# The second table's last four tiles multiplied feature by feature, and another pace for the gathered rows' steps

## The chip, the cores and the metric

The kernel runs on one core of one Trainium2 chip. The metric is the device time of one execution in microseconds (us). Three runs of the kernel before gave 2100.40, 2096.53 and 2106.97 us; their median is 2100.4 us.

## The reference, cut to what matters

The program is two stacks one behind the other: two mixer layers, then two layers that each hold a mixer (HGRN2 in the first, RG-LRU in the second) and a PEER feed-forward part. The change touches the PEER part alone, which is computed twice, once per layer:

```
q = (h @ w_q) -> 8 heads, two halves each; scores against 128 sub-keys; top 16 of each half,
top 16 of their 256 sums: ids (16384 experts), gate = softmax(top_s)
u = u_tab[ids]; act = gelu(sum_d u * h)
out = sum over heads and the 16 picks of (gate * act) * v_tab[ids]
x = x + g2 * out
```

There are 256 tokens, 1024 features and two tables of 16384 x 1024 numbers (64 MB each) per layer. All data are float32.

## The kernel before, in words

Two ways of computing the PEER part stand side by side. For 160 of the 256 tokens (`TD`) it is dense: every tile of the tables is multiplied with all 160 tokens. For the other 96 (`TS`) only the picked rows are fetched, by indirect DMAs on GpSimd's queue, and VectorE multiplies and sums them.

**The second table's dense part** (line 1452). The table v is cut into 128 tiles of 128 experts. For tile j the kernel runs eight matmuls, one for each block c of 128 output features; each adds into a PSUM region of its own (`acc[c // 2][:, c % 2]`), its right operand is the 160 tokens' weights `W(j)`. In the trace one such float32 matmul shows as two records. Two tiles come in one load of 1 MB, called a pair here, on SyncE's queue into one of four buffers `w`; the load of a pair can be issued when the matmuls of the pair four before it are done.

**The gathered rows** (lines 1302 to 1332, `fetch` and `own`). Steps k = 0 to 95 gather rows of the first table, steps 96 to 191 rows of the second. One `fetch(k)` brings 128 rows (512 KB) into one of twelve buffers `r`; one `own(k)` on VectorE multiplies them with their weights and adds them to a sum `hl` of 128 x 1024. Each 32 steps fill one sum, so there are three in the second table: steps 96 to 127, 128 to 159 and 160 to 191. The first step of a sum is a plain product (line 1330), the other 31 are line 1332.

**The joins** (line 1446). When a sum is full, eight matmuls per join (16 records) add it, folded from slots to tokens, into the other 96 columns of the same PSUM regions. A join stands in TensorE's queue at a fixed place: `folds[j + 5]`, five tiles behind the tile at which its last step was written down. TensorE works in order, so a join that waits holds up every matmul behind it.

**The order.** The whole stage stands in `manual_schedule()`: instructions go out as written. The condition in line 1455, with the factor 122, says behind which tile j the next step k is written; and `fetch(k + 6, ends[j - 1])` lets the fetch start only when tile j - 1 is multiplied. With 122 the 96 steps go from tile 2 to tile 123, about one per 1.27 tiles, and the joins stand behind tiles 47 and 88 and behind the last tile.

**The end of the stage.** Behind the last join eight evictions (VectorE and ScalarE in turn, lines 1471 and 1473) take the PSUM regions to `hT` and scale them; sixteen transposes (line 1478) turn them back, four to a PSUM tile; four sums (line 363) add them to x. Then the next stage begins: the RG-LRU mixer behind the first PEER part, the final norm behind the second. The mixer's weight loads (`lruin`, `lruax`, line 243, into buffers `r`; `ada`, line 222, into buffers `w`) are issued on SyncE's queue as buffers come free.

Of the kernel before, what the change touches and what calls it, by code (L numbers as in the profile page):

```python
# [15 lines left out]
AF = mybir.ActivationFunctionType  # L16
ALU = mybir.AluOpType
AX = mybir.AxisListType

P = 128  # L20
# [7 lines left out]
TS = 96  # L28
# [109 lines left out]
class Kernel:  # L138
# [1053 lines left out]
    def peer(self, l):  # L1192
        from contextlib import ExitStack
        nc, tc, A = self.nc, self.tc, self.A
        pairs = {}

        def load(name, j):
            if j % 2 == 0:
                pairs[name] = self.slot(A[f"{name}{l}"][:, j * D:(j + 2) * D])
            return pairs[name][:, j % 2 * D:(j % 2 + 1) * D]  # L1200

        with ExitStack() as ctx:
            pool = lambda name, bufs=1, c=ctx: c.enter_context(tc.tile_pool(name=f"{name}{l}", bufs=bufs))
            pl = pool("pe")
            hT = self.t(pl, (P, 8, S), "hT")
# [100 lines left out]
            def fetch(k, behind=None):  # L1306

                if k < 2 * TS:
                    x = self.rp.tile([P, D], F32, name="r")
                    at = bass.IndirectOffsetOnAxis(ap=ids[:, k % TS:k % TS + 1], axis=0)  # L1310
                    g = nc.gpsimd.indirect_dma_start(out=x, out_offset=None, in_=A[f"urow{l}"] if k < TS else vrow,  # L1311
                                                     in_offset=at)
                    if behind is not None:
                        tc.add_manual_dep(g.ins, behind.name, mybir.DependencyInfo(
                            mybir.DependencyClass.Sync, mybir.DependencyReason.ANTI), reason="pace")
                    rows[k] = x

            def own(k):

                g, r = k % TS, k % TS // 32  # L1320
                x = rows.pop(k)
                if k < TS:
                    nc.vector.scalar_tensor_tensor(x, x, 1.0, hrep[r % 2], op0=ALU.mult, op1=ALU.mult,  # L1323
                                                   accum_out=asl[:, g:g + 1])
                    if k % 32 == 31:
                        gr = slice(32 * r, 32 * r + 32)
                        nc.scalar.activation(asl[:, gr], asl[:, gr], AF.Gelu_apprx_tanh)
                        nc.vector.tensor_tensor(asl[:, gr], asl[:, gr], gs[:, gr], op=ALU.mult)
                elif g % 32 == 0:
                    nc.vector.tensor_scalar(accs[r % 2], x, asl[:, g:g + 1], None, op0=ALU.mult)  # L1330
                else:
                    nc.vector.scalar_tensor_tensor(accs[r % 2], x, asl[:, g:g + 1], accs[r % 2], op0=ALU.mult,  # L1332
                                                   op1=ALU.add)

            with tc.manual_schedule():
                wts = {}

                def W(j):
                    return Wa[:, j] if j < JW else wts["b"][:, j - JW]
# [56 lines left out]
                k = 0  # L1396
                for j in range(P):
                    u_mm(j)
                    if j in (2, 29):
                        b = j // 29  # L1400
# [28 lines left out]
                    if j >= G0:  # L1429
                        n = j - G0  # L1430
# [10 lines left out]
                acc = [self.t(self.acc, (P, 2, S), "acc") for _ in range(4)]  # L1441
                ends, folds = [], {}

                def join(r):
                    for c in range(8):
                        nc.tensor.matmul(acc[c // 2][:, c % 2, :TS], accs[r % 2][:, c * P:(c + 1) * P], fold[:, r],  # L1446
                                         start=False, stop=r == NR - 1, skip_group_check=True)

                for j in range(P):
                    v = load("v", j)  # L1450
                    for c in range(8):
                        mm = nc.tensor.matmul(acc[c // 2][:, c % 2, TS:], v[:, c * P:(c + 1) * P], W(j),  # L1452
                                              start=j == 0 and c % 2 == 0, stop=False, skip_group_check=True)
                    ends.append(mm.ins)
                    if k < 2 * TS and (j - 2) * TS >= (k - TS) * 122:
                        own(k)
                        fetch(k + AHEAD, ends[j - 1])
                        k += 1
                        if k % 32 == 0:
                            folds[j + 5] = (k - TS) // 32 - 1  # L1460
                    if j in folds:
                        join(folds.pop(j))
                assert k == 2 * TS
                for r in folds.values():
                    join(r)

            g0 = 24 + 16
            for c in range(8):
                gate = self.mod[l][:, g0 + c:g0 + c + 1]
                if c % 2:  # L1470
                    nc.scalar.activation(hT[:, c], acc[c // 2][:, c % 2], AF.Copy, scale=gate)  # L1471
                else:
                    nc.vector.tensor_scalar(hT[:, c], acc[c // 2][:, c % 2], gate, None, op0=ALU.mult)  # L1473
            for b in range(2):
                for n in range(2):
                    ps = self.psum((P, 4, P))
                    for j in range(4):
                        nc.tensor.transpose(ps[:, j], hT[:, 4 * n + j, b * P:(b + 1) * P], self.ident)
                    self.add_x(b, n, ps.rearrange("p a b -> p (a b)"), None)

    def final(self, out):
        nc = self.nc
        rows = self.wp.tile([P, SLOT], F32, name="w")[:, :D]
        r = self.A["rows"]
        nc.scalar.dma_start(rows, bass.AP(tensor=r.tensor, offset=r.offset + R_FINAL, ap=[[0, P], [1, D]]))
        for b in range(2):
            o = self.rp.tile([P, D], F32, name="r")
            rs = self.rms_x(b)
            nc.vector.tensor_scalar(rs, rs, float(D) ** 0.5, None, op0=ALU.mult)
            nc.vector.scalar_tensor_tensor(o, self.x[:, b], rs, rows, op0=ALU.mult, op1=ALU.mult)  # L1490
            nc.sync.dma_start(out[b * P:(b + 1) * P], o)
# [38 lines left out]
```

## Time and profile before

| what | value |
|---|---|
| median of three runs | 2100.4 us |
| profiled execution, its own time | 2102.61 us |
| its span from first to last instruction | 2100.9 us |
| TensorE busy | 1998.1 us, 95% of the span |
| VectorE / ScalarE / GpSimd busy | 67% / 29% / 30% |
| granted TensorE clock, mean | 0.979 of full speed |
| line 1452 (second table, dense), both layers | 4096 records, 558.0 us |
| DMA | 630 MB, mean 300 GB/s |

How to read it: a group's row gives the time its records are on the engine, the mean duration of one, and behind the bar how long the engine stood idle just before them and what ended that. Matmul records overlap, so what one costs in a row of them is read from the chain of waits (time over count), not from its duration. The DMA share is the mean busy share of the 16 DMA engines.

### The profile page before, as it was taken

What the parts mean: (1) busy time and instruction counts of PE and PEld (TensorE: products, weight loads), DVE (VectorE), ACT (ScalarE), POOL (GpSimd) and SP (SyncE); (2) the same over time, 40 slices, a digit from 0 to 9 for tenths busy, and PEclk for the clock granted to TensorE, in tenths of its full rate; (3) what the DMA queues carried; (4) which work ended last, traced back from release to release, by engine and by line L of the source; (5) the groups of instructions that cost most, each with busy time, mean ns of one, the idle gap of its engine ahead of it and who ended that gap; (6) DMA issues with size and microseconds to landing.
All of it is one profiled execution on the core that took longest, in us unless ns stands there. A gap on an engine that the chain in (4) does not pass through costs nothing. (4 is left out here: it accounts for less than half of the span.)

```text
span 2100.9 us, 35398 instructions
## 1 busy us (share of the span) xinstructions
PE 1998.1 (95%) x13860; PEld 1871.6 (89%) x13860; DVE 1403.3 (67%) x3068; ACT 617.7 (29%) x1684; POOL 626.3 (30%) x683
## 2 busy tenths in 40 slices
PE   6997998999999989999999998999989999999997
PEld 6683795888769989999999998969989999999997
DVE  7698588577657777788444446976796788544344
ACT  4452472455433134433000002743224433000000
POOL 0201111011001564443343440001374444243442
PEclk9998999999999999999999998999999999999999
DMA  9647738442414999999999998643799999999996
GB/s 343 233 160 265 262 111 310 149 123 71 161 61 157 356 405 364 358 365 363 381 415 416 415 415 338 243 180 120 294 404 377 353 366 372 356 416 416 415 415 270
DMA packets 123719, 630.01 MB, mean 300 GB/s; under 512 B 13728, under 2 KB 14368, under 8 KB 79264
## 3 DMA queue, kind: packets, MB, share of 16 engines
q1 hardware_dynamic: 66960, 422.87, 52.5%
q0 software_dynamic: 55296, 201.35, 24.6%
q10 hardware_dynamic: 1296, 3.53, 0.5%
q8 instruction: 109, 1.79, 0.3%
q14 instruction: 58, 0.48, 0.1%
HBM read 626.65 MB, written 1.05 MB: 299 GB/s over the span
## 5 line engine op out<-in xcount | busy, mean ns | idle before, releaser
L1353 PE MATMUL ps<-hT,w 128*128 128x160 f32 x4096 | 574.8, 300 | 0.0
L1353 PEld LDWEIGHTS ps<-hT,w 128*128 128x128 f32 x4096 | 562.4, 191 | 0.0
L1332 DVE SCALAR_TENSOR_TENSOR hl<-r,asl,hl 128x1024 f32<-128x1024 f32 x186 | 239.0, 1285 | 314.8 <-DMA r<-v,ids 314.2
L1452 PE MATMUL acc<-Wa,w 128*128 128x160 f32 x2560 | 348.4, 299 | 0.0
L1452 PEld LDWEIGHTS acc<-Wa,w 128*128 128x128 f32 x2560 | 347.9, 190 | 0.0
L1311 POOL DMA_INDIRECT r<-v,ids x192 | 232.0, 1208 | 346.4 <-PE acc L1452 255.1
L1311 POOL DMA_INDIRECT r<-urow,ids x192 | 252.7, 1316 | 243.3 <-DVE r L1323 133.6
L1323 DVE SCALAR_TENSOR_TENSOR r<-r,hh 128x1024 f32<-128x1024 f32 x192 | 231.9, 1218 | 2.2 <-DMA r<-urow,ids 1.9
L1452 PE MATMUL acc<-Wb,w 128*128 128x160 f32 x1536 | 209.6, 299 | 0.2 <-DMA w<-v 0.2
L1452 PEld LDWEIGHTS acc<-Wb,w 128*128 128x128 f32 x1536 | 208.8, 190 | 0.5 <-DMA w<-v 0.5
L1471 ACT ACTIVATE hT<-acc,mod 128x256 f32<-128x256 f32 x8 | 3.7, 475 | 569.6 <-DVE hT L1473 569.6
L1373 ACT ACTIVATE r<-r,hl 128x128 f32<-128x128 f32 x320 | 102.3, 391 | 233.7 <-DVE r L1370 233.7
L257 PE MATMUL ps<-hh,r 128*128 128x256 f32 (+1 forms) x464 | 135.9, 293 | 4.6 <-ACT r L229 2.9
L259 PE MATMUL ps<-hh,r 128*128 128x256 f32 (+1 forms) x464 | 133.6, 288 | 6.6 <-DVE r L230 6.6
L258 PE MATMUL ps<-hl,r 128*128 128x256 f32 (+1 forms) x464 | 133.7, 288 | 1.0 <-DVE hl L381 1.0
L270 DVE SCALAR_TENSOR_TENSOR w<-w,crow 128x1024 f32<-128x1024 f32 x96 | 113.6, 1216 | 3.2 <-ACT crow L835 3.2
L230 DVE TENSOR_TENSOR r<-w,r 128x1024 fp32r<-128x1024 f32 (+1 forms) x82 | 97.5, 1199 | 27.2 <-ACT r L229 26.2
L229 ACT ACTIVATE r<-w 128x1024 fp32r<-128x1024 f32 (+1 forms) x82 | 84.3, 1039 | 77.8 <-PE ps L258 34.3
L1370 DVE TENSOR_TENSOR r<-cst,hl 128x1024 f32<-128x1024 f32 x80 | 97.4, 1218 | 0.0
L259 PEld LDWEIGHTS ps<-hh,r 128*128 128x128 f32 (+1 forms) x464 | 89.0, 192 | 7.9 <-DVE r L230 7.6
L257 PEld LDWEIGHTS ps<-hh,r 128*128 128x128 f32 (+1 forms) x464 | 89.5, 193 | 6.2 <-ACT r L229 3.8
L258 PEld LDWEIGHTS ps<-hl,r 128*128 128x128 f32 (+1 forms) x464 | 89.3, 193 | 2.1 <-DVE hl L381 1.6
(382 smaller groups left out, 2910.0 us busy)
## 6 DMA issues: line engine op xcount, KB each, us to landing
w<-u SPq DMA_DIRECT2D x128, 1024.0 KB, 8.0
w<-v SPq DMA_DIRECT2D x128, 1024.0 KB, 8.3
w<-ada SPq DMA_DIRECT2D x48, 1024.0 KB, 4.9
w<-win SPq DMA_DIRECT2D x24, 1024.0 KB, 5.0
r<-hgin SPq DMA_DIRECT2D x40, 512.0 KB, 4.4
w<-wq SPq DMA_DIRECT2D x12, 1024.0 KB, 5.0
r<-wout SPq DMA_DIRECT2D x16, 512.0 KB, 8.6
r<-wmid SPq DMA_DIRECT2D x12, 384.0 KB, 7.6
```

Source lines behind the costliest of these rows:

```text
L230: self.nc.vector.tensor_tensor(lo, x, hi.bitcast(F32), op=ALU.subtract)
L257: mm(ps, a[0], b[0], start=start, stop=False)
L258: mm(ps, a[0], b[1], start=False, stop=False)
L259: mm(ps, a[1], b[0], start=False, stop=stop)
L270: nc.vector.scalar_tensor_tensor(x, x, 1.0, self.cond, op0=ALU.mult, op1=ALU.mult, accum_out=m[:, j + i:j + i + 1])
L1311: g = nc.gpsimd.indirect_dma_start(out=x, out_offset=None, in_=A[f"urow{l}"] if k < TS else vrow, in_offset=at)
L1323: nc.vector.scalar_tensor_tensor(x, x, 1.0, hrep[r % 2], op0=ALU.mult, op1=ALU.mult, accum_out=asl[:, g:g + 1])
L1332: nc.vector.scalar_tensor_tensor(accs[r % 2], x, asl[:, g:g + 1], accs[r % 2], op0=ALU.mult, op1=ALU.add)
L1353: nc.tensor.matmul(ps, u[:, c], hT[:, c, TS:], start=c == 0, stop=c == 7)
L1370: nc.vector.tensor_tensor(o, self.iota[:, None, None].to_broadcast([P, 2, 4, P]), slots[:, 1:3, k:k + 4, None].to_broadcast([P, 2, 4, P]), ...
L1373: nc.scalar.activation(o[:, 1, t], o[:, 1, t], AF.Copy, scale=slots[:, 0, k + t:k + t + 1])
L1452: mm = nc.tensor.matmul(acc[c // 2][:, c % 2, TS:], v[:, c * P:(c + 1) * P], W(j), start=j == 0 and c % 2 == 0, stop=False, skip_group_che ...
```

## The change

It has two parts. First, the pace: the factor 122 becomes 114, so the 96 steps go from tile 2 to tile 115, one per 1.19 tiles, and all three joins stand inside the loop over tiles, which now ends with tile 123. Second, the last four tiles (124 to 127) are both loaded, and then multiplied feature block by feature block: for each c the four tiles' matmuls, then the eviction of c. Behind the blocks 5, 6 and 7 stand a group of four transposes and its sum into x, and one more group behind that. The order of the four groups is now (token half 0, features 0 to 511), (half 1, the same), (half 0, features 512 to 1023), (half 1, the same). Evictions, transposes and sums are inside `manual_schedule()` now.

```diff
-                for j in range(P):
+                def v_mm(j, v, c):
+                    return nc.tensor.matmul(acc[c // 2][:, c % 2, TS:], v[:, c * P:(c + 1) * P], W(j),
+                                            start=j == 0 and c % 2 == 0, stop=j == P - 1, skip_group_check=True)
+
+                LAST = 4
+                for j in range(P - LAST):
                     v = load("v", j)
                     for c in range(8):
-                        mm = nc.tensor.matmul(acc[c // 2][:, c % 2, TS:], v[:, c * P:(c + 1) * P], W(j),
-                                              start=j == 0 and c % 2 == 0, stop=False, skip_group_check=True)
+                        mm = v_mm(j, v, c)
                     ends.append(mm.ins)
-                    if k < 2 * TS and (j - 2) * TS >= (k - TS) * 122:
+                    if k < 2 * TS and (j - 2) * TS >= (k - TS) * 114:
                         own(k)
                         fetch(k + AHEAD, ends[j - 1])
...
-                assert k == 2 * TS
-                for r in folds.values():
-                    join(r)
+                assert k == 2 * TS and not folds
+                vs = [load("v", j) for j in range(P - LAST, P)]
+                turns = [(b, n) for n in range(2) for b in range(2)]
...
+                for c in range(8):
+                    for j in range(P - LAST, P):
+                        v_mm(j, vs[j - P + LAST], c)
+                    gate = self.mod[l][:, g0 + c:g0 + c + 1]
+                    if c % 2:
+                        nc.scalar.activation(hT[:, c], acc[c // 2][:, c % 2], AF.Copy, scale=gate)
+                    else:
+                        nc.vector.tensor_scalar(hT[:, c], acc[c // 2][:, c % 2], gate, None, op0=ALU.mult)
+                    if c in (5, 6, 7):
+                        turn(*turns[c - 5])
+                turn(*turns[3])
```

TensorE's queue in the second table of one layer, in the kernel before: line 1452 are the dense matmuls (eight to a tile), line 1446 a join, line 1478 the transposes, `Wa` and `Wb` the weights of the first 80 and the last 48 tiles.

```order
L1452 MATMUL acc<-Wa,w 128x160 x384
L1446 MATMUL acc<-fold,hl 128x96 x8
L1452 MATMUL acc<-Wa,w 128x160 x256
L1452 MATMUL acc<-Wb,w 128x160 x72
L1446 MATMUL acc<-fold,hl 128x96 x8
L1452 MATMUL acc<-Wb,w 128x160 x312
L1446 MATMUL acc<-fold,hl 128x96 x8
L1478 MATMUL ps<-cst,hT 128x128 x16
```

The same place in the changed kernel; dense matmuls are line 1450 there, transposes line 1477, and eight more transposes follow.

```order
L1450 MATMUL acc<-Wa,w 128x160 x360
L1446 MATMUL acc<-fold,hl 128x96 x8
L1450 MATMUL acc<-Wa,w 128x160 x280
L1450 MATMUL acc<-Wb,w 128x160 x24
L1446 MATMUL acc<-fold,hl 128x96 x8
L1450 MATMUL acc<-Wb,w 128x160 x304
L1446 MATMUL acc<-fold,hl 128x96 x8
L1450 MATMUL acc<-Wb,w 128x160 x48
L1477 MATMUL ps<-cst,hT 128x128 x4
L1450 MATMUL acc<-Wb,w 128x160 x4
L1477 MATMUL ps<-cst,hT 128x128 x4
L1450 MATMUL acc<-Wb,w 128x160 x4
```

The joins move from behind tiles 47, 88 and 127 (384, 712 and 1024 matmuls) to behind tiles 44, 82 and 120 (360, 664 and 968), and eight of the sixteen transposes move ahead of the last blocks' matmuls.

SyncE's queue of loads at the end of the first layer's second table: `w<-v` are pairs of tiles, `r<-lruin` and `w<-ada` loads of the next stage. Rows with a minus stand in the kernel before, with a plus in the changed one.

```order
-L222 DMA w<-v 128x2048 x62
+L222 DMA w<-v 128x2048 x58
 L243 DMA r<-lruin 128x1024
 L222 DMA w<-v 128x2048
 L243 DMA r<-lruin 128x1024
 L222 DMA w<-v 128x2048
-L243 DMA r<-lruin 128x1024 x2
+L243 DMA r<-lruin 128x1024
+L222 DMA w<-v 128x2048
+L243 DMA r<-lruin 128x1024
+L222 DMA w<-v 128x2048 x3
 L222 DMA w<-ada 128x2048 x4
```

The first four loads of the mixer's weights move ahead of four pairs; each of them waits for a buffer `r` that a late step of the gathered rows gives free.

## Rows read from the trace of the kernel before

**Rows 1.** Chain of waits, second layer's second table: start us, us, what.
```profile
1804.75 104.32 PE acc L1452 x768
...
2086.51 1.76 PE acc L1446 x16
```
**Rows 2.** Busy time by stretch: start:end, us, then engines; last granted clock, DMA share, GB/s.
```profile
1810.00:1820.00 10.00, 10.00 (x76) 10.00 (x75) 3.93 (x4) 0.00 (x0) 3.68 (x4) 1.00 0.83 286
1830.00:1960.00 130.00, 130.00 (x963) 130.00 (x961) 56.16 (x45) 0.00 (x0) 51.42 (x46) 1.00 1.02 416
1960.00:2070.00 110.00, 110.00 (x815) 110.00 (x814) 45.70 (x36) 0.00 (x0) 49.66 (x37) 1.00 1.02 415
2070.00:2080.00 10.00, 10.00 (x76) 10.00 (x75) 5.14 (x4) 0.00 (x0) 0.00 (x0) 1.00 0.95 388
2080.00:2090.00 10.00, 10.00 (x80) 9.72 (x79) 6.78 (x9) 1.81 (x4) 0.00 (x0) 1.00 0.08 31
```
**Rows 3.** DMA queues and issues, 1830 to 2070 us: MB and share; KB, us to landing.
```profile
q1 hardware_dynamic: 7837, 57.12, 57.4%
q0 software_dynamic: 11626, 42.33, 44.1%
...
w<-v SPq DMA_DIRECT2D x55, 1024.0 KB, 8.3
r<-v,ids POOLq DMA_INDIRECT x82, 20.1
```
**Rows 4.** VectorE in order of time, second layer: start, duration, shapes, idle before and releaser.
```profile
1898.62 1.28 DVE L1332 SCALAR_TENSOR_TENSOR hl<-r,asl,hl 128x1024 f32<-128x1024 f32 x1 [1.85 <-DMA r<-v,ids]
...
1986.30 1.28 DVE L1332 SCALAR_TENSOR_TENSOR hl<-r,asl,hl 128x1024 f32<-128x1024 f32 x1 [1.85 <-DMA r<-v,ids]
...
1995.42 1.29 DVE L1332 SCALAR_TENSOR_TENSOR hl<-r,asl,hl 128x1024 f32<-128x1024 f32 x1 [1.54 <-DMA r<-v,ids]
...
2080.57 3.93 DVE L1332 SCALAR_TENSOR_TENSOR hl<-r,asl,hl 128x1024 f32<-128x1024 f32 x3 [0.71 <-DMA r<-v,ids]
```
**Rows 5.** The dense matmuls by their line: ns min/median/max, first and last start.
```profile
L1452 PE MATMUL acc<-Wa,w x2560: 299/299/328, 996.2 to 1980.1; 128*128 128x160 f32 x197
```
**Rows 6.** VectorE and TensorE in order of time, first layer.
```profile
1185.70 1.29 DVE L1332 SCALAR_TENSOR_TENSOR hl<-r,asl,hl 128x1024 f32<-128x1024 f32 x1 [1.22 <-DMA r<-v,ids]
1188.85 0.75 DVE L1330 TENSOR_SCALAR hl<-r,asl 128x1024 f32<-128x1024 f32 x1 [1.86 <-DMA r<-v,ids]
...
1247.06 1.28 DVE L1332 SCALAR_TENSOR_TENSOR hl<-r,asl,hl 128x1024 f32<-128x1024 f32 x1 [2.20 <-DMA r<-v,ids]
...
1280.52 1.28 DVE L1332 SCALAR_TENSOR_TENSOR hl<-r,asl,hl 128x1024 f32<-128x1024 f32 x1 [2.17 <-DMA r<-v,ids]
1281.86 2.86 PE L1446 MATMUL acc<-fold,hl 128*128 128x96 f32 x16 [3.28 <-DVE hl L1332]
...
1286.78 1.89 DVE L363 TENSOR_TENSOR x<-ps,x 128x512 f32<-128x512 f32 x3 [0.26 <-PE ps L1478]
```
**Rows 7.** TensorE in order of time, after its longest wait in the second layer.
```profile
1564.30 1.97 PE L1299 MATMUL ps<-cst,r 128*128 128x128 f32 x8 [8.67 <-ACT r L1295]
```
**Rows 8.** Chain of waits just behind it, and 15 us later.
```profile
1566.26 6.03 PE ps L1353 x32
...
1581.66 4.35 PE ps L1353 x32
```
**Rows 9.** Busy time by stretch there; third from last the granted clock.
```profile
1560.00:1570.00 10.00, 5.70 (x25) 5.71 (x26) 9.93 (x20) 2.54 (x5) 7.36 (x6) 0.52 1.02 415
```
**Rows 10.** SyncE's queue in order of time, end of the first layer's second table.
```profile
1265.09 13.85 SPq L222 DMA_DIRECT2D w<-ada  x4
```
**Rows 11.** All engines in order of time, end of the second layer.
```profile
2087.48 1.81 ACT L1471 ACTIVATE hT<-acc,mod 128x256 f32<-128x256 f32 x4 [282.39 <-DVE hT L1473]
2088.10 2.02 PE L1478 MATMUL ps<-cst,hT 128*128 128x128 f32 x16
2088.87 2.61 DVE L363 TENSOR_TENSOR x<-ps,x 128x512 f32<-128x512 f32 x4
```

More of the change, by code (lines that the diff above doesn't have):

```diff
@@ L1462, in peer, with turn @@
                         join(folds.pop(j))
-                assert k == 2 * TS
-                for r in folds.values():
-                    join(r)
[L1467 to L1475, printed above, removed]
+                assert k == 2 * TS and not folds
+                vs = [load("v", j) for j in range(P - LAST, P)]
+                g0 = 24 + 16
+                turns = [(b, n) for n in range(2) for b in range(2)]
+                def turn(b, n):
                     ps = self.psum((P, 4, P))
```

## The prediction

> **What bounds the kernel now.** I read the chain of waits at the second table first. In the second layer it is TensorE alone: 768 records of line 1452 in 104.32 us [rows 1], 0.1358 us each, so a tile (16 records) takes 2.173 us and 128 tiles 278.2 us; the three joins, 1.76 us each, stand between them (the chain shows no wait ahead of the last). Then busy time by stretch: from 1830 to 2070 us TensorE is busy without a gap at the full clock (1.00, the 2.4 GHz level), and at the same time the DMA engines are busy with a share of 1.02 at 415 to 416 GB/s [rows 2]. So two limits lie on each other. The table by queues says who shares the DMA engines: in 240 us q1 (mostly tiles of v) moves 57.1 MB, 238 GB/s, and q0 (gathered rows) 42.3 MB, 176 GB/s [rows 3]. TensorE eats a pair of 1.05 MB in 4.35 us, 241 GB/s; the tiles get what they need, the rows get the rest, 0.524 MB in 2.97 us. The pace of 122 asks for one in 2.173 x 122/96 = 2.76 us, faster than they come. VectorE in order of time confirms it: its steps are idle before and ended by the row's landing [rows 4, 6], and a fetch takes 20.1 us in the median against 8.3 us of a pair twice its size [rows 3]. The rows are bound by the DMA engines' rate, not by the pace; the joins have just waited late enough for them.
>
> **The pace and the joins.** The change asks for rows earlier, every 2.58 us, from engines that have nothing to give. Only before 1820 us is there room (share 0.83 from 1810 to 1820 [rows 2]), and there the two paces write their steps 97 to 99 behind the same tiles. So I take the rows' landings as they were until something else stops. The joins, in TensorE's in-order queue, come earlier.
>
> Second layer, first matmul 1804.75. Join 0 behind tile 44: 1804.75 + 45 x 2.173 = 1902.5; its last step, 127, is over at 1898.62 + 1.28 = 1899.9 [rows 4]. It fits with 2.6 us; cost 0, at most 2. Join 1 behind tile 82: 1804.75 + 83 x 2.173 + 1.76 = 1986.9; its last step, 159, is over at 1995.42 + 1.29 = 1996.7 [rows 4]. TensorE would stand 9.8 us. That is the upper end, since the standing TensorE asks for no tiles and the rows get their share. The lower end: at 1986.3 step 156 has started [rows 4], three rows of 0.524 MB are out; at 415 GB/s for rows alone 3.8 us, and 1.4 us for the step: 1991.5, a wait of 4.6. Between them I take 7.7: with a pair issued each 4.35 us and 8.3 us to landing two pairs are under way, an estimated 1.3 MB, that go on taking turns and cost 3.1 us more. Behind the waiting join stand all later matmuls, and behind those the buffers of v.
>
> First layer, first matmul 996.2 [rows 5]: join 1 is reached at 996.2 + 180.4 + 1.8 = 1178.4, step 159 (ahead of the plain product of step 160, at 1188.85) is over at 1187.0 [rows 6], a wait of up to 8.6; less the same 2.1, 6.5 us.
>
> **The clock behind a wait.** A wait of 8.67 us in the second layer [rows 7] was followed by the low level: granted 0.52 from 1560 to 1570 us [rows 9], 1.2 GHz for nearly all of it, counting the wait. The records behind it: 32 of line 1353 in 6.03 us, against 4.35 later [rows 8], and eight of line 1299 in 1.97, about 0.98 too much at half speed: 2.7 us. For a shorter wait the join of the first layer is the nearest: 3.28 us of idle, then 2.86 us for 16 records that take 1.76 [rows 6, 1], 1.1 us. I take 2.7 for each join 1; bounds 1.1 and 2.7.
>
> **Join 2 and what is late next.** Delayed by 7.7 + 2.7 = 10.4, TensorE reaches join 2 behind tile 120 at 1804.75 + 121 x 2.173 + 3.5 + 10.4 = 2081.6. Step 191 was over at 2080.57 + 3.93 = 2084.5 [rows 4]; 10.4 us without tiles leave 2.5 MB for rows, 6.0 us of the engines: 2078.5. No wait; bound 2.9. In the first layer the join is reached at 996.2 + 262.9 + 3.5 + 9.2 = 1271.8; step 191 was over at 1281.8 [rows 6], less 5.3 by the same sum, and less up to 5 because four loads of `ada`, issued from 1265.09 before [rows 10], now find no free buffer before the join. That is 1271.5 to 1276.5, a wait of 0 to 4.7; I take 2.
>
> **SyncE's queue.** The first load of `lruin` now stands ahead of pair 58 and waits for step 180, over at 1248.3 (twentieth behind the plain product at 1188.85 [rows 6]). Pair 58 could go when tile 109 is done, 996.2 + 239.0 + 3.5 + 9.2 = 1247.9. Cost 0, hidden by join 1's delay. Without that delay it would be 9.6 us late, and the 4.7 us by which a pair is ahead (three pairs, 13.0, less 8.3) would leave 4.9 us of starving.
>
> **The end of the stage.** Before, from the last join's end, 2088.27 [rows 1], to the last sum's, 2088.87 + 2.61 = 2091.48 [rows 11], 3.2 us pass: evictions and transposes follow the join block by block and hardly leave TensorE idle. Now eight transposes, 2.02/16 = 0.126 us each [rows 11], stand ahead of the last matmul: 1.0 us on the path. Behind it one eviction (1.81/4 = 0.45), four transposes (0.5), two sums (2 x 0.65) and some 0.45 us of handovers (an estimate): 2.7. Net +0.5 per layer; bounds -1 and +1.5. The blockwise order of the 64 matmuls costs nothing: same records, both pairs long landed.
>
> **The sum.** First layer: 278.2 + 5.3 (joins) + 1.0 + 6.5 + 2.7 + 2.0 + 2.7 = 298.4, so x is done at 1294.6; before at 1286.78 + 1.89 = 1288.7 [rows 6], which holds a wait of 3.3 and a slow join, both gone. +5.9. Second layer: 278.2 + 5.3 + 1.0 + 7.7 + 2.7 + 2.7 = 297.6, x at 2102.4 against 2091.5: +10.9. Together +16.8 on the profiled execution's 2102.61: 2119.4. The median of three runs lies 2.2 lower: **2117**.
>
> **A page's figure against this.** The Trainium skill (DMA: Bandwidth & Descriptors, "Where 436 GB/s comes from") puts the ceiling at 435 GB/s, from 16 SBUF ports. By it the rows would have 194 GB/s left and come every 2.70 us; from step 127 at 1898.6 step 159 would then start at 1985.0, end at 1986.3, and join 1 would not wait: the case of the other side below, 2097. The trace does not bear it out for this mix: two long stretches stand at 415 and 416 with a share of 1.02 [rows 2].
>
> **Rivals.**
> *Half of it (2109).* Join 1 hardly waits, because more waiting rows win a larger share: the tiles' lead of 4.7 us is 1.1 MB, two rows, 6.0 us sooner, which leaves waits of 1.7 and 0.5. Then the loss comes at join 2, and the engines' rate bounds it there from below. A delay D gives the rows 0.57 D (238 of 415 GB/s), so D is at least (2084.5 - 2071.2)/1.57 = 8.5 us in the second layer, if they worked at full rate to the end. They did not: from 2070 to 2080 at 388 GB/s, and from 2080 on only 31 [rows 2], so the bytes could have been there some 3.1 us sooner (0.31 MB left at 2080 against 0.28 missed before, and the last step starts about 2083.2 [rows 4]). With that D is 6.5; likewise in the first layer, with the 5 us of `ada`, (1281.8 - 5 - 3.1 - 1262.6)/1.57 = 7.1. Without a fall of the clock: +6.5 + 0.5 and 7.1 + 0.5 - 4.4 (the old wait of 3.3 and slow join of 1.1), +10.2; with the lead spent on top, up to 2.5 less in each layer and +5.2. Between them +8, so 2109 with the median. For it: nothing but the engines' bytes is certain to hold a join back. Against it: pairs come 8.3 us behind their issue whether few or many fetches are out, so the rows don't win a share. The skill (same page, "Queues, rings and completion order") has each DMA engine take turns between its queues, by which a longer queue gets no more turns; the stretches before and after 1960, with one rate and no gap in TensorE, agree.
> *On the other side (2097).* The rows come sooner with the earlier request, as if pace were their limit: no join waits. Then the first layer loses its 3.3 + 1.1 us of waiting and each end costs between -1 and +0.5: -3.4 at the middle, 2097. It decides if a row comes at least every 2.7 us; against it stands VectorE's idle time, ended by landings 20 us behind their issue [rows 3].
> *Everything late (2126).* Join 1 waits its full 9.8 and 8.6 us, join 0 waits 2 with a slow join, and join 2 in the first layer 4.7: +4.2, +3.1 and +2.7 on the forecast, less what one delay takes from the next: 2126. For it: step 127 has 2.6 us to spare, less than one row's interval.
> *The change does not do what it says:* excluded by the order, joins are behind tiles 44, 82 and 120.
>
> **How the numbers follow.** Forecast 0.62, half of it 0.21, other side 0.05, everything late 0.12. The range holds the low bounds of the forecast's waits (4.6 and 3.4 at join 1, 1.1 behind each, nothing at the first layer's join 2: -11.4, 2106), nearly all of the second case, and the fourth: 2103 to 2128; the forecast alone 2109 to 2124. A measurement of this kernel tells about 0.5%, 10.5 us, from no change. Slower than 2110.9: nine tenths of the forecast, a fifth of the second, the fourth: 0.72. Faster than 2089.9: the other side with both tails at -1 reaches only 2094, so 0.03. The rest, 0.25.
>
> **What would show it.** Right: TensorE idle ahead of the join behind tile 82, 5 to 10 us in both layers, ended by line 1332 on VectorE, the granted clock near 0.5 behind it, the DMA share still 1.0 at 415 GB/s up to there, step 159 within 3 us of where it was. Wrong: a join 1 without a wait, rows landing every 2.7 us or less, waits for `w<-v` in place of the joins' waits, or most of the loss at join 2.

## The result, and the profile after

The changed kernel takes 2124.02 us (median of 4 runs, 2121.61 to 2125.53) against 2101.16 us of the kernel before in the same comparison: ratio 1.0096, 95% interval 1.0078 to 1.0114. It is about 1% slower. The forecast was 2117 us, with a range of 2103 to 2128.

The profiled execution took 2122.86 us, its span is 2121.1. Where the time went is read by stage: from the first matmul of the second table (999.5 and 1811.6 us) to the last sum into x (1299.4 and 2111.7). That is 299.9 us in the first layer and 300.1 in the second, against 292.5 and 286.9 before [rows 5, 6, 1, 11]: +7.4 and +13.2, together 20.6. The rest of the difference lies in stages that the change does not touch (last section).

The chain of waits of the changed kernel, second layer (start us, us, what):

```profile
1951.07 25.85 DMA r<-v,ids
...
1977.70 22.77 DMA r<-v,ids
...
2000.57 1.29 DVE hl L1332
...
2001.91 3.73 PE acc L1446 x16
2005.64 83.01 PE acc L1450 x608
2088.65 1.76 PE acc L1446 x16
2090.41 7.65 PE acc L1450 x56
```

Before, the chain ran on TensorE alone through this stage [rows 1]. Now it goes back from join 1 over step 159 to two fetches, one behind the other, that are under way for 25.9 and 22.8 us. TensorE in order of time at the two joins 1, first and second layer (start, duration, idle before and its releaser):

```profile
1188.99 3.73 PE L1446 MATMUL acc<-fold,hl 128*128 128x96 f32 x16 [7.20 <-DVE hl L1332]
```

```profile
2001.91 3.73 PE L1446 MATMUL acc<-fold,hl 128*128 128x96 f32 x16 [7.99 <-DVE hl L1332]
```

Waits of 7.20 and 7.99 us; the 16 records behind them take 3.73 us instead of 1.76. Joins 0 and 2 wait for nothing in either layer. Busy time by stretch around the second one (third from last the granted clock, then DMA share and GB/s):

```profile
1837.00:1990.00 153.00, 153.00 (x1132) 153.00 (x1131) 63.87 (x51) 0.00 (x0) 68.35 (x53) 1.00 1.02 416
1990.00:2001.00 11.00, 3.92 (x29) 3.67 (x28) 5.41 (x5) 0.00 (x0) 5.61 (x4) 0.78 1.02 413
2001.00:2011.00 10.00, 9.09 (x54) 9.10 (x55) 9.29 (x8) 0.00 (x0) 6.36 (x5) 0.73 1.03 409
2011.00:2080.00 69.00, 69.00 (x510) 69.00 (x509) 30.84 (x25) 0.00 (x0) 23.78 (x20) 1.00 1.01 407
```

While TensorE stands, the DMA engines are as full as ever, 1.02 at 413 GB/s, as in [rows 2], but the tiles' queue q1 moves only 1.19 MB in the 8 us from 1994 to 2002, 149 GB/s instead of 238 [rows 3]. The clock falls to the 1.2 GHz level in the wait and stays there for 4.4 us behind it (the means of 0.78 and 0.73 hold parts at either level). The end of the second layer, all engines in order of time:

```profile
2098.08 0.48 DVE L1488 TENSOR_SCALAR hT<-acc,mod 128x256 f32<-128x256 f32 x1 [15.62 <-PE acc L1450]
2098.62 2.20 PEld L1450 LDWEIGHTS acc<-Wb,w 128*128 128x128 f32 x16 [0.82 <-DVE hT L1488]
2098.62 2.44 PE L1450 MATMUL acc<-Wb,w 128*128 128x160 f32 x16 [0.58 <-DVE hT L1488]
2100.01 0.47 ACT L1486 ACTIVATE hT<-acc,mod 128x256 f32<-128x256 f32 x1 [287.93 <-PE acc L1450]
2101.10 0.48 DVE L1488 TENSOR_SCALAR hT<-acc,mod 128x256 f32<-128x256 f32 x1 [2.54 <-PE acc L1450]
2101.64 2.20 PEld L1450 LDWEIGHTS acc<-Wb,w 128*128 128x128 f32 x16 [0.82 <-DVE hT L1488]
...
2110.40 1.29 DVE L363 TENSOR_TENSOR x<-ps,x 128x512 f32<-128x512 f32 x2 [1.70 <-PE ps L1477]
```

A pair of blocks begins every 3.02 us (2098.62, 2101.64), though its 16 records take 16 x 0.1358 = 2.17 us. TensorE waits for VectorE's eviction of an even block before it begins the odd one. I had not forecast that.

### The profile page after: what moved, and what is told of

Same layout as the page of the kernel before. It is cut to its first block, busy times and chain, and to the rows that moved or that the text cites. A ratio compares the mean times of both kernels' runs of the same rounds, so it can differ in the third digit from the quotient of the medians.

```text
span 2121.1 us, 35400 instructions
## 1 busy us (share of the span) xinstructions
PE 2001.6 (94%) x13860; PEld 1872.3 (88%) x13860; DVE 1402.6 (66%) x3068; ACT 616.5 (29%) x1684; POOL 636.5 (30%) x683
## 5 line engine op out<-in xcount | busy, mean ns | idle before, releaser
L1311 POOL DMA_INDIRECT r<-v,ids x192 | 240.5, 1253 | 314.6 <-PE acc L1450 198.5
```

## The experiments

The theory: the DMA engines' rate binds the gathered rows, so a join that comes earlier waits; and the blocks of one PSUM tile wait for each other's evictions. In the stage lengths below the first number is the first layer's, the second the second layer's. A ratio is to the kernel before in the same comparison: 2104.1 us in the first four experiments, 2101.94 in the next two, 2102.53 in the last two.

**Asking earlier, without needing earlier.**

```diff
-                    if k < 2 * TS and (j - 2) * TS >= (k - TS) * 122:
+                    if k < 2 * TS and (j - 2) * TS >= (k - TS) * 114:
...
-                            folds[j + 5] = (k - TS) // 32 - 1
+                            r = (k - TS) // 32 - 1
+                            folds[(47, 88, P)[r]] = r
```

> The kernel before with the pace of 114, its joins left behind tiles 47, 88 and the last, its end as it was: rows are asked for earlier and nobody needs them earlier. Theory (the DMA engines' rate binds the rows): rows land as before; in the second layer from the first matmul of the second table to the last sum into x 286.9 us as before, within 1; in the first layer 292.5 within 4, because SyncE's queue now has loads of the next stage ahead of four pairs there and may starve TensorE up to 4.9 us; time 2099 to 2105. Rival (the pace binds the rows): rows land some 8 us sooner at the end, the first layer's wait of 3.3 us goes, time 2096.

Measured: 2106.74 us, ratio 1.0016 (1.0001 to 1.0032), 1.7 us above the expected range. Second layer 286.9; counted from its first matmul, step 159 is over at 190.3 us (before 192.1, and 190.4 in a second profile of the kernel before) and step 191 at 280.0 (before 279.9). The new pace lets the last fetch go behind tile 107, at 238 us; it went at 260.4 as in the kernel before, because GpSimd's queue by then waits for earlier fetches to land. So in the second layer rows come no sooner, and not the pace binds them. That the engines' bytes do, and not the number of fetches that can be under way, this run alone does not show; the fifth experiment bears on it. The first layer takes 295.2, and its profile shows the starving that the prediction's step on SyncE's queue had priced at 4.9 us without join 1's delay. SyncE's queue, then TensorE:

```profile
1237.50 0.33 SPq L222 DMA_DIRECT2D w<-v  x1
1248.22 0.33 SPq L243 DMA_DIRECT2D r<-lruin  x1
1248.64 0.38 SPq L222 DMA_DIRECT2D w<-v  x1
```

```profile
1260.29 1.97 PE L1452 MATMUL acc<-Wb,w 128*128 128x160 f32 x6 [5.43 <-DMA w<-v]
```

Pair 58 is issued 11 us behind pair 57, right behind the first load of `lruin`, which waited for its buffer `r`; pairs otherwise follow each other in 4.35 us. TensorE stands 5.4 us for a tile. In this layer the rows do come sooner, as the rival had it: step 191 is over at 275.5 us from the first matmul instead of 285.6, and the last join no longer waits. But 11 us without an issue of a pair left bytes to the rows, and the first `ada` load goes out 8 us later than before, counted from the first matmul (1276.10 here, 1265.09 in [rows 10]); so this layer does not tell the theories apart. Nothing is gained by it: the last join ends at 292.0 us from the first matmul instead of 288.5.

**The joins' part alone.** The same change of the pace, the joins written as the rule has them, the end of the kernel before.

```diff
-                    if k < 2 * TS and (j - 2) * TS >= (k - TS) * 122:
+                    if k < 2 * TS and (j - 2) * TS >= (k - TS) * 114:
```

> The kernel before with the pace of 114 and so with its joins behind tiles 44, 82 and 120, but with its own end (tiles to 127 in order, evictions, transposes and sums behind them). Theory: the waits at join 1 stay at 7 and 8 us with 2.5 us of slow clock behind each, and only the end of the changed kernel goes, which costs some 2.5 to 3 us per layer over this one: second layer 297, first layer 297 from first matmul to last sum, time 2118. Rival (the end has a part in the join's wait, or costs nothing): time as the changed kernel's, 2124.

Measured: 2117.63 us, ratio 1.0069 (1.0048 to 1.0091); stages 296.9 and 297.4, with waits of 6.15 and 7.77 us at join 1. TensorE at join 1 of the second layer:

```profile
2000.07 3.73 PE L1446 MATMUL acc<-fold,hl 128*128 128x96 f32 x16 [7.77 <-DVE hl L1332]
```

The wait and the slow records are there without the new end. In the second layer 10.5 us of 13.2 belong to the early joins, 2.7 to the end. Counted from the start of join 2 to the last sum, the old end takes 20.5 us and the new one 23.2 in both layers.

**Blocks in another order.**

```diff
-                for c in range(8):
+                for i, c in enumerate((0, 2, 1, 3, 4, 6, 5, 7)):
                     for j in range(P - LAST, P):
                         v_mm(j, vs[j - P + LAST], c)
...
-                    if c in (5, 6, 7):
-                        turn(*turns[c - 5])
+                    if i in (5, 6, 7):
+                        turn(*turns[i - 5])
```

> The changed kernel with its last blocks in the order 0, 2, 1, 3, 4, 6, 5, 7, so that two blocks of one PSUM tile do not follow each other (except where nothing else is left). Theory (the 0.58 us in which TensorE stands ahead of each odd block, with its weight load behind, is the wait for the even block's eviction out of the same PSUM tile): the three waits of 0.58 us and most of the fourth go, 0.85 us each on the path: 2.5 to 3.4 us per layer, second layer 297, time 2118. Rival (an eviction hinders TensorE whichever tile it reads, or the blocks are slow for another reason): second layer stays at 300, time 2124.

Measured: stages 296.8 and 297.2. The first six blocks go through without a gap; TensorE, VectorE and ScalarE in order of time, second layer:

```profile
2086.75 10.76 PE L1450 MATMUL acc<-Wb,w 128*128 128x160 f32 x78
...
2092.11 0.48 DVE L1488 TENSOR_SCALAR hT<-acc,mod 128x256 f32<-128x256 f32 x1 [15.54 <-PE acc L1450]
2093.20 0.48 DVE L1488 TENSOR_SCALAR hT<-acc,mod 128x256 f32<-128x256 f32 x1 [0.61 <-PE acc L1450]
2094.28 0.47 ACT L1486 ACTIVATE hT<-acc,mod 128x256 f32<-128x256 f32 x1 [288.20 <-PE acc L1450]
```

Evictions run beside the matmuls as before, only not out of the tile that is written: every wait of TensorE of 0.58 us for line 1488 is gone, and from join 2 to the last sum both layers take 20.3 us instead of 23.2. So it is the shared PSUM tile (`acc[c // 2]`), not an eviction as such. Whether the kernel could do without the wait was not tested. The median, 2121.44 us with 2113.94 to 2122.27 in 4 runs (ratio to before 1.0091, 1.0064 to 1.0118), lies between what the two theories gave and is too spread to tell 6 us, the difference of the two stages together; the stages decide.

**The first two joins back, the third early.**

```diff
-                            folds[j + 5] = (k - TS) // 32 - 1
+                            r = (k - TS) // 32 - 1
+                            folds[(47, 88, 120)[r]] = r
```

> The changed kernel with the first two joins moved back to behind tiles 47 and 88, the third still behind tile 120. Theory (the bytes of all rows bound the third join if no earlier wait has given them time): no wait at joins 0 and 1, a wait of 10 to 13 us at join 2 in the second layer and about as much in the first, the slow clock behind it; second layer 301 to 304 from first matmul to last sum, time 2122 to 2130: the loss moves and does not go. Rival (only join 1 is too early, the rest fits): no wait at any join, 290 us, time 2104.

Measured: 2128.79 us, ratio 1.0127 (1.0100 to 1.0154); stages 299.0 and 304.4. The second layer's join 2:

```profile
2089.96 3.73 PE L1446 MATMUL acc<-fold,hl 128*128 128x96 f32 x16 [11.66 <-DVE hl L1332]
```

No wait at joins 0 and 1, 11.66 us at join 2, and the slow clock again: the loss moves to where the rows are next asked for too early, and it is larger. The last pair was issued at 2076.2 us, ahead of the wait that begins at 2078.3, so a standing TensorE gives the rows no turn of a tile load here, as it did at join 1. Nor is all of the wait the engines': they move 409 GB/s from 2078 to 2084 and 119 from then to 2090. The last 5.2 us are four steps of VectorE in a row, behind the landing that ended its own wait:

```profile
2084.66 5.25 DVE L1332 SCALAR_TENSOR_TENSOR hl<-r,asl,hl 128x1024 f32<-128x1024 f32 x4 [1.23 <-DMA r<-v,ids]
```

In the first layer the expectation missed: TensorE starved 5.6 us for a pair behind the `lruin` loads, as in the first experiment, and join 2 then waited only 0.3.

**Fewer bytes for the tiles.** One pair in eight is not loaded; its matmuls use the pair before it.

```diff
-            if j % 2 == 0:
+            if j % 2 == 0 and not (name == "v" and j % 16 == 14):
                 pairs[name] = self.slot(A[f"{name}{l}"][:, j * D:(j + 2) * D])
```

> The changed kernel, but one pair of tiles of the second table in eight is not loaded: its matmuls use the pair before it again, so the output is not the reference's. Theory (bytes bind the rows): tiles ask for 211 instead of 241 GB/s, the rows have 204 and come every 2.57 us, as fast as they are asked for; in the second layer join 1 and join 2 wait for nothing, the slow clock behind join 1 goes, and from the first matmul to the last sum it takes 290 us (300.1 less 8.0 and 2.3); time near 2105. Rival (the rows are bound by their own queue, the way of a fetch or VectorE's steps, whatever the tiles load): join 1 still waits 7 to 8 us, 300 us, time 2122.

Measured: 2105.76 us, ratio 1.0011 (0.9994 to 1.0029); stages 289.75 in both layers. TensorE at join 1 of the second layer, and the DMA queues and issues from 1830 to 2070 us:

```profile
1986.85 1.92 PE L1446 MATMUL acc<-fold,hl 128*128 128x96 f32 x16
```

```profile
q1 hardware_dynamic: 6919, 50.34, 52.0%
q0 software_dynamic: 12188, 44.34, 46.4%
...
r<-v,ids POOLq DMA_INDIRECT x82, 12.1
```

No idle time ahead of the join; step 159 is over at 169.9 us from the first matmul instead of 190.3. q1 gave up 6.8 MB against [rows 3], and a fetch lands in 12.1 us instead of 20.1. Nothing of the rows' own way was changed, so what held them was the tiles' bytes beside them. Whether more fetches under way at once would take a larger share from the tiles was not tested. What is left over the kernel before, 2.9 us in the second layer, is the new end.

**Holding back the next stage's loads,** on the kernel before: the first load of `ada` in the mixer waits for step 191.

```diff
-        self.nc.sync.dma_start(x, src)
+        self.loaded = self.nc.sync.dma_start(x, src)
...
+            if getattr(self, "hold", None) is not None:
+                self.tc.add_manual_dep(self.loaded.ins, self.hold.ins.name, mybir.DependencyInfo(
+                    mybir.DependencyClass.Sync, mybir.DependencyReason.ANTI), reason="hold")
+                self.hold = None
...
-                    nc.vector.scalar_tensor_tensor(accs[r % 2], x, asl[:, g:g + 1], accs[r % 2], op0=ALU.mult,
-                                                   op1=ALU.add)
+                    o = nc.vector.scalar_tensor_tensor(accs[r % 2], x, asl[:, g:g + 1], accs[r % 2], op0=ALU.mult,
+                                                       op1=ALU.add)
+                    if k == 2 * TS - 1:
+                        self.hold = o
```

> The kernel before with one more wait: the next stage's loads of ada, which go out from 1265 us on while the first layer's last rows are still under way, wait for the last step of the rows. Theory (the engines' bytes bind the last join of the first layer too): its rows come some 4 to 5 us sooner, the wait of 3.3 us ahead of the last join and its slow records go, 288 instead of 292.5 us from first matmul to last sum, the mixer behind begins at the full clock; time 4 to 7 us shorter, 2097 to 2100 where the kernel before has 2104. Rival (the rows' landing there is not a matter of other loads): 292.5 us as before; or the loads held back are late for the mixer, and it takes longer by what was gained.

Measured: 2101.35 us, ratio 0.9992 (0.9979 to 1.0006); first layer 288.4 us, and its last join:

```profile
1286.11 2.02 PE L1452 MATMUL acc<-fold,hl 128*128 128x96 f32 x16 [0.79 <-DVE hl L1336]
```

Before it waited 3.28 us and took 2.86 [rows 6]. The stage is as short as expected, but the 4 to 7 us of time did not show: the time is not told from the kernel before.

**Both once more.** The kernel before, unchanged, and the one just shown.

> The kernel before, unchanged, to see how far a second profile of it differs. Theory (the first 1000 us, which no kernel here changes, vary by some us from run to run): the first layer's second table begins anywhere from 996 to 1003 us, the stage from its first matmul to the last sum takes 292.5 and 286.9 us again, within 1. Rival (the stage's own length varies by several us too): 288 to 296 in the first layer.

> The kernel with the held loads of ada once more. Theory: 288.4 us in the first layer and the mixer behind it 4 us shorter as in its first profile, whatever the beginning does; the time some 4 to 8 us below that of the kernel before if the beginning is alike. Rival: the gain in one profile is a matter of that run, and the stage takes 292 us in this one.

Measured: 2101.52 us, ratio 0.9990 (0.9975 to 1.0004), for the kernel before against itself, stages 290.5 and 286.9; 2100.69 us, ratio 0.9991 (0.9977 to 1.0005), for the held loads, stages 287.4 and 286.9. The first layer's stage varies by 2 us in the kernel before (expected was within 1), so the held loads save 2 to 5 us there in two profiles each; in the time they don't show. The 4 us of the mixer, which the last expectation took over from the first profile, did not come again: the stretch from the first layer's last sum to the second layer's first matmul takes 511.6 and 514.1 us with held loads, 515.9 and 511.8 without (last section). No version was found that is measurably faster than the kernel before.

## Why the prediction was right, step by step

*What bounds the stage:* right, and shown: earlier requests alone change nothing in the second layer, fewer tile bytes end the waits. How the engines divide their rate between the two queues was read from the rows and not tested.

*Join 0:* forecast 0, measured 0. *Join 1:* forecast 6.5 and 7.7 us, measured 7.20 and 7.99. The bounds, 3.4 to 8.6 and 4.6 to 9.8, held; pairs under way do keep the rows back as estimated: q1 moved 1.19 MB in the second wait, where the estimate was 1.3. *The clock:* forecast 2.7 for each; from the delay of the matmuls behind the join over that ahead of it, less the wait, 2.6 and 2.4.

*Join 2:* forecast 2 and 0, measured 0 and 0. With about 10 us of time given at join 1 the last step is over at 271.4 and 270.9 us from the first matmul, 276.7 and 276.9 is the join. That it would wait without a loss at join 1 is shown by the fourth experiment, 11.66 us; the rival "half of it" had 6.5 to 8.5 there, too little.

*SyncE's queue:* forecast 0 behind a delayed join 1, 4.9 us without; measured 0.3 in the changed kernel (one wait for `w<-v` in the first layer), and 5.4 and 5.6 in the two kernels with all tile loads whose join 1 did not wait.

*The end of the stage:* this step failed. "The blockwise order of the 64 matmuls costs nothing: same records" left out that two blocks share a PSUM tile, and that an eviction of one now stands ahead of the matmuls of the other; in the kernel before all matmuls and joins were written ahead of all evictions. These waits cost 2.9 us per layer (third experiment), and the rest of the new end next to nothing where 0.5 was forecast: the new end as a whole costs 2.7 us (against the second experiment) to 2.9 (the fifth against the kernel before), outside its bounds of -1 to +1.5.

*The sum:* stage by stage +5.9 was forecast for the first layer and +7.4 measured, +10.9 and +13.2 for the second: 16.8 against 20.6. The two ends are short by 4.4 to 4.7 us in all; join 1 and the clock behind it measured 0.6 more than forecast, the wait for a tile 0.3, and the 2 us of join 2 did not come: together 3.3 to 3.6 of that difference of 3.8. It is luck that the 2 us of join 2 hide part of the end's error. Direction, place and mechanism were right, the size was short by one term. The median lies 7 us above the forecast, at the upper edge of the 2109 to 2124 that the forecast alone allowed; what these terms don't explain of it, some 3 us, lies outside the two stages, in the spread of the last section. In the rival on the other side "-3.4 at the middle" is a slip: -4.4 and two ends at the middle of -1 to +0.5 give -4.9, and -3.4 is the upper end.

*The figure of 435 GB/s* that the prediction weighed, from the Trainium skill (DMA: Bandwidth & Descriptors, "Where 436 GB/s comes from"): no long stretch of this stage reaches it here; with tiles and rows both asking it is 416 GB/s in the changed kernel too. Join 1 waited, which by that figure it would not have done.

## What to carry to other kernels

When a transfer lands long behind its issue while the DMA engines are full, as the rows do here, asking earlier alone may move nothing; what counts is the bytes due before each place that waits, so a waiting place may only be moved ahead as far as they allow. An edit that mixes evictions with matmuls needs a look at which PSUM tile each of them touches: records that cost the same in another order can wait for each other. And where a queue is shared, a load that moves ahead in it takes its own wait with it, to everything that stands behind.

## What was not expected of the hardware

The stage from tile to sum repeats within 0.1 us in the second layer (286.9 us in five profiles of three kernels without early joins), yet the first matmul of the first layer's second table begins anywhere from 996.2 to 1003.0 us in ten profiles whose matmuls up to there are the same. This spread, not the stage, limits what the times can tell: 20.6 us in the two stages stand beside 22.9 us between the medians, and 2 to 5 us in one stage did not show in 23 runs.

The spread goes with the granted clock. Summed over the trace's record of it, the low level of 1.2 GHz holds for 51.2 us ahead of that first matmul in the two earliest profiles (996.2 and 997.0 us), for 54.6 to 58.0 us in five that begin at 999.0 to 999.5, and for 64.9 to 68.3 us in the three from 1001.3 on.

The stretch behind the first layer's stage, up to the second layer's second table, differs with the clock too. It took 511.6 to 512.2 us in five profiles with 17.1 us at the low level, the changed kernel's among them; 513.1 and 513.4 with 20.5; 514.1 with 23.9; and 515.9 in two with 27.3. The unchanged kernel alone has both ends: 515.9 us, with 10.2 us at the low level right behind the last sum, and 511.8, with 3.4. So the 4 us that this stretch was shorter in the first profile with held loads are no gain of theirs. Why the clock is low for longer in one execution than in another is not shown.
